# Two plain feed-forward blocks by token half, and the activation sums on GpSimd

## The chip, the core and the metric

The kernel runs on one NeuronCore of a Trainium2 chip. The metric is the device time of one execution in microseconds; the time given is the median of the runs. A change of 0.2% is about what the measurement can tell from no change.

## The reference

One layer of a diffusion backbone over 1024 latent tokens of width 1024 (and 256 context tokens). A modulated RMS norm and a projection feed two groups of heads, a bidirectional gated DeltaNet and a neighbourhood attention; their outputs go through one projection and a gated residual. The last part, which this case is about, is a second modulated RMS norm and a SwiGLU feed-forward with inner width 2816, with another gated residual:

```
x = x + g1 * (jnp.concatenate([dn_x, na_x], axis=-1) @ w_out[i])
x = x + g2 * swiglu(modulate(rms_norm(x, norm2_w[i]), sh2, sc2), w_ffn_in[i], w_ffn_out[i])

def swiglu(h, w_in, w_out):
    gate, up = jnp.split(h @ w_in, 2, axis=-1)
    return (jax.nn.silu(gate) * up) @ w_out
```

All inputs are float32.

## The kernel before

Activations are kept transposed: 128 partitions hold 128 of the 1024 features, the free axis holds tokens. The 1024 tokens are two halves of 512 (HV), because one matmul output is a bank of 128x512. Products of float32 values are made from rounded parts: every operand is split into hi (rounded, made on ScalarE) and lo (the rest, a subtraction on VectorE), and a product is three matmuls, hi*hi, hi*lo and lo*hi. A helper, product (L1206), issues for one weight pair and one 512x512 quarter of the activations 4 x 3 x 2 = 24 matmuls of 128x512 into two banks (L1212).

The normed activations form a 2x2 grid of quarters B11, B12, B21, B22: the first index is the half of the features, the second the half of the tokens. quadrant (L1394) makes one quarter: four times a scaling by weight and norm factor on VectorE (L1398), a shift on ScalarE (L1399), and the split (L1391 on ScalarE, L1392 on VectorE). The norm factor rs of a token half comes from normed (L1303): a matmul with ones over the sum of squares (L1306), then a logarithm and an exponential on ScalarE (L1307, L1308), each with a table load. finish (L1296) adds the last two feature rows of the residual for one half and updates the sum of squares (L1328, L1333, L1334).

The feed-forward's 22 blocks of 128 inner columns use two schemes. The first two blocks (PLAIN = 2) take gate and up columns with the quarters directly: eight products of 24 matmuls, in the order block 0 first half, block 0 second half, block 1 first half, block 1 second half. The other twenty go in pairs through a seven-product scheme on the 2x2 grid (L1491 to L1524), which needs four more activation tiles T1 to T4, sums of the quarters. sums (L1402) makes these while the second plain block runs: sixteen 128x512 subtractions (L1410, in place in the unsplit quarters) and their splits. T4 takes the buffers of B12.

Weights come through Stream: a raw tile wq by DMA on SyncE's queue (L1245), for some a sum ws of raw tiles on VectorE (L1269), then the pair uhi (ScalarE, L1273) and ulo (VectorE, L1274), six buffers each. make produces one pair; next takes two, gate and up; ahead(n) makes pairs until n are waiting. Around the plain blocks, a background generator, late, steps the modulation of the last gate (L231, L233, loads of wad) on VectorE; its result is used after the seven-product blocks. In the plain blocks, activation and product of gate and up are L1463 (ScalarE, SiLU) and L1464 (VectorE, reading the banks in PSUM).

The source order is not the order on the engines. The Tile framework traces the program and then schedules it: each engine gets its own order, from source priority and estimated ready times, with waits on the tiles' producers and on the last readers of a buffer that is used again. On the chip every engine then runs its own list in order.

## Time and profile before

| | us |
|---|---|
| median of 3 runs | 1626.84 |
| lowest and highest run | 1625.8, 1627.12 |
| profiled execution | 1629.29 |
| its span, first to last instruction | 1627.4 |
| mean granted TensorE clock | 0.974 |

The profile is of one execution. PE is TensorE's matmuls, PEld its weight loads, DVE VectorE, ACT ScalarE, POOL GpSimd, SPq SyncE's queue of DMA issues. Times in a timeline are from the start of the span; a bracket at the end of a row gives the idle time of the engine before it and what ended that. In a group of instructions, the numbers behind the bar are busy time, mean length of one in nanoseconds, and idle time before.

### The profile page before, as it was taken

How to read it: one execution, taken by the hardware profiler on the slowest of the kernel's cores; microseconds unless marked ns; L12 is line 12 of the kernel's file. 1: busy time of each engine (PE TensorE's matmuls, PEld its weight loads, DVE VectorE, ACT ScalarE, POOL GpSimd, SP SyncE). 2: the span in 40 equal slices, each digit the busy share in tenths (PEclk: the TensorE clock that was granted, in tenths of full speed). 3: DMA queues.
4: the chain of work that ended last, by engine and by line, in shares of the span. 5: the costliest groups of instructions: out<-in, count | busy, mean ns of one | idle time of the engine just before them, and what ended most of it. 6: DMA issues, size and time to landing. Idle time of an engine off the chain costs nothing.

```text
span 1627.4 us, 24128 instructions
## 1 busy us (share of the span) xinstructions
PE 1518.4 (93%) x8642; PEld 1278.9 (79%) x8642; DVE 1044.0 (64%) x1935; ACT 706.3 (43%) x1337; POOL 199.5 (12%) x271
## 2 busy tenths in 40 slices
PE   2999899999988897999998999999999999999999
PEld 1789787779888785788776787888888888888887
DVE  4785678544364466577897638876665666679752
ACT  4443363663332234565665227333333333445441
POOL 0144611422333320000010000000000000000000
PEclk9898999999999899999998999999999999999999
DMA  9266121545345537999955910533222323698742
GB/s 371 85 214 211 56 75 40 179 125 188 104 139 199 175 102 200 310 283 286 269 168 160 312 70 33 181 111 104 98 97 97 110 98 118 226 361 308 260 158 84
DMA packets 211719, 275.22 MB, mean 169 GB/s; under 512 B 16144, under 2 KB 120080, under 8 KB 210576
## 3 DMA queue, kind: packets, MB, share of 16 engines
q1 hardware_dynamic: 205552, 268.34, 51.0%
q10 hardware_dynamic: 6048, 5.35, 1.0%
q8 instruction: 68, 1.11, 0.3%
q14 instruction: 51, 0.42, 0.1%
HBM read 206.78 MB, written 71.04 MB: 171 GB/s over the span
## 4 chain that ended last, share of the span: by engine, by line
PE 74%; DVE 10%; DMA 7%; ACT 5%; issue 2%; POOL 2%; SPq 0%; ACTq 0%; DVEq 0%; POOLq 0%
PE ps L1212 26%; PE ps L1559 13%; PE blk L388 10%; PE blk L571 4%; PE ps L1343 3%; PE pr L913 3%; PE sc L317 2%; PE sc L307 2%; PE sc L295 2%; DMA wad<-wa 1%; DVE N L819 1%; DMA at<-qk_d 1%; DVE tt L817 1%; PE ps L1105 1%; PE pr L904 1%
## 5 line engine op out<-in xcount | busy, mean ns | idle before, releaser
L388 PE MATMUL blk<-hh,whi 128*128 128x512 f32 (+1 forms) x416 | 124.4, 391 | 3.6 <-ACT hh L683 3.3
L1273 ACT CAST uhi<-ws 128x512 fp32r<-128x512 f32 x91 | 54.7, 622 | 151.2 <-PE ps L1212 76.8
L1273 ACT CAST uhi<-wq 128x512 fp32r<-128x512 f32 x101 | 60.6, 621 | 136.0 <-issue 61.3
L388 PE MATMUL blk<-hh,wlo 128*128 128x512 f32 (+1 forms) x416 | 118.5, 378 | 0.6 <-POOL wlo L199 0.6
L388 PE MATMUL blk<-hl,whi 128*128 128x512 f32 (+1 forms) x416 | 117.9, 376 | 0.9 <-DVE hl L685 0.9
L1274 DVE TENSOR_TENSOR ulo<-wq,uhi 128x512 fp32r<-128x512 f32 x101 | 67.4, 688 | 66.7 <-ACT uhi L1273 35.6
L1212 PE MATMUL ps<-hT,uhi 128*128 128x512 f32 x336 | 104.6, 393 | 3.1 <-ACT hT L1391 3.1
L1212 PE MATMUL ps<-lT,uhi 128*128 128x512 f32 x336 | 104.0, 391 | 0.0
L1212 PE MATMUL ps<-hT,ulo 128*128 128x512 f32 x336 | 103.9, 390 | 0.0
L1212 PE MATMUL ps<-hB,uhi 128*128 128x512 f32 x288 | 89.7, 392 | 0.0
L571 PE MATMUL blk<-zhi,hh 128*128 128x256 f32 (+2 forms) x304 | 89.5, 294 | 0.0
L1212 PE MATMUL ps<-lB,uhi 128*128 128x512 f32 x288 | 89.3, 391 | 0.0
L1212 PE MATMUL ps<-hB,ulo 128*128 128x512 f32 x288 | 89.1, 390 | 0.0
L571 PE MATMUL blk<-zhi,hl 128*128 128x256 f32 (+2 forms) x304 | 88.2, 290 | 0.0
L571 PE MATMUL blk<-zlo,hh 128*128 128x256 f32 (+2 forms) x304 | 87.4, 288 | 0.0
L388 PEld LDWEIGHTS blk<-hh,wlo 128*128 128x128 f32 x416 | 73.9, 192 | 16.0 <-issue 1.6
L388 PEld LDWEIGHTS blk<-hl,whi 128*128 128x128 f32 x416 | 74.0, 193 | 15.5 <-DVE hl L685 1.2
L388 PEld LDWEIGHTS blk<-hh,whi 128*128 128x128 f32 x416 | 71.9, 195 | 17.6 <-issue 3.6
L1274 DVE TENSOR_TENSOR ulo<-ws,uhi 128x512 fp32r<-128x512 f32 x91 | 60.8, 687 | 37.5 <-ACT uhi L1273 29.2
L198 ACT CAST whi<-wraw 128x1024 fp32r<-128x1024 f32 x26 | 27.3, 1049 | 119.1 <-PE blk L388 56.9
L1212 PEld LDWEIGHTS ps<-hT,uhi 128*128 128x128 f32 x336 | 63.3, 189 | 16.5 <-ACT hT L1391 3.5
L1212 PEld LDWEIGHTS ps<-hT,ulo 128*128 128x128 f32 x336 | 63.4, 189 | 13.3
(331 smaller groups left out, 3751.9 us busy)
## 6 DMA issues: line engine op xcount, KB each, us to landing
wq<-w_fo SPq DMA_DIRECT2D x99, 256.0 KB
wq<-w_gu SPq DMA_DIRECT2D x88, 256.0 KB
wad<-wa SPq DMA_DIRECT2D x64, 256.0 KB
bt<-rpb SPq DMA_DIRECT2D x64, 192.0 KB
t_d<-g SPq DMA_DIRECT2D x22, 512.0 KB
fr<-t_d SPq DMA_DIRECT2D x44, 256.0 KB
f_d<-g SPq DMA_DIRECT2D x33, 256.0 KB
fr<-f_d SPq DMA_DIRECT2D x33, 256.0 KB
```

What stands on the lines that cost most here:

```text
L198: act.copy(h, r)
L295: pe.matmul(sc[:, u * 640 + n0:u * 640 + n1], q, ks[i], start=i == 0, stop=i == 1)
L307: pe.transpose(sc[:, u * 640 + j * 128:u * 640 + (j + 1) * 128], bt[:, j * 128:(j + 1) * 128], ident)
L317: pe.matmul(sc[u * ND:u * ND + ND, 1280:1408], vv, pt[:, j * 128:(j + 1) * 128], start=j == 0, stop=j == 4)
L388: pe.matmul(o, ww[:, k], xx[k][:, s], start=k == 0 and j == 0, stop=k == KT - 1 and j == 2)
L571: pe.matmul(p[:, :c1 - c0], x[k][:, s], ww[:, k, c0:c1], start=k == 0 and j == 0, stop=k == KT - 1 and j == 2)
L913: pe.matmul(p[:, hs[h]], f[:, h], src[:, h], start=True, stop=True)
L1212: pe.matmul(o, w[wi][:, k], x[xi][:, k], start=first and k == 0 and j == 0, stop=k == n - 1 and j == 2, skip_group_check=True)
L1273: act.copy(hi, self.raw[key])
L1274: dve.tensor_tensor(lo, self.raw[key], hi.bitcast(F32), OP.subtract)
L1343: pe.matmul(o, w[wi][:, k], parts[xi][k][:, s], start=k == 0 and j == 0, stop=k == KT - 1 and j == 2)
L1559: pe.matmul(o[b], w[wi][:, b], F[xn, p][xi], start=n in (0, 1, 5) and p == 0 and j == 0, stop=p == NFB // 2 - 1 and j == 2, skip_group_che ...
```

## The change

The two plain blocks are run by token half: both blocks over the first half, then both over the second. The ones-matmul for the second half's norm factor is issued inside the second product, after its first quarter, and the quarters B12 and B22 are made after the first block's first half, as before. All eight weight pairs of the two blocks stay in their buffers until the second half has used them, so uhi and ulo get eight buffers each instead of six; the space that the kernel reserves for DMA descriptors shrinks to 1024 bytes. The sixteen subtractions that make T1 to T4 go from VectorE to GpSimd; their splits stay on ScalarE and VectorE. They are issued beside the four products of the second half. The background modulation takes no steps in the first pair of the seven-product blocks.

```
-    def product(outs, ws, x, first=True):
+    def product(outs, ws, x, first=True, between=None):
...
+            if between and k == 0:
+                between()
...
-            hi = uw.tile([128, 4, 128], F32R, name="uhi", tag="uhi", bufs=6)
-            lo = uw.tile([128, 4, 128], F32R, name="ulo", tag="ulo", bufs=6)
+            hi = uw.tile([128, 4, 128], F32R, name="uhi", tag="uhi", bufs=8)
+            lo = uw.tile([128, 4, 128], F32R, name="ulo", tag="ulo", bufs=8)
...
-                    dve.tensor_tensor(B[at][:, k], B[x][:, k], B.get(y, B["B11"])[:, k], OP.subtract)
+                    pool.tensor_tensor(B[at][:, k], B[x][:, k], B.get(y, B["B11"])[:, k], OP.subtract)
...
-        for f in range(PLAIN):
-            po = [[bank(), bank()] for _ in range(2)]
-            g = prev[f]
-            w = [up.next(), None]
-            for t in range(2):
-                for i in range(2):
-                    if f == 0 and t == 1 and i == 0:
-                        for n in ("B12", "B22"):
-                            quadrant(n)
-                    if t == 0 and i == 1:
-                        w[1] = up.next()
-                    product([po[0][t], po[1][t]], w[i], X[f"B{i + 1}{t + 1}"], i == 0)
-                    if f == 0 and t == 0:
-                        if i == 0:
-                            normed(1)
-                        up.ahead(4)
-                    elif f:
-                        for _ in range(4):
-                            next(todo, 0)
-                        up.ahead(4)
-                act.activation(g[:, t], po[0][t], AF.Silu)
-                dve.tensor_tensor(g[:, t], po[1][t], g[:, t], OP.mult)
+        w = [[], []]
+        for t, f in ((0, 0), (0, 1), (1, 0), (1, 1)):
+            po, g = [bank(), bank()], prev[f]
+            for i in range(2):
+                if t == 0:
+                    w[f].append(up.next())
+                product(po, w[f][i], X[f"B{i + 1}{t + 1}"], i == 0,
+                        (lambda: normed(1)) if (t, f, i) == (0, 0, 1) else None)
+                if t == 0 and f == 0:
+                    up.ahead(2 + 2 * i)
+                elif t == 0 and i == 0:
+                    up.ahead(2)
+                elif t == 1:
+                    for _ in range(4):
+                        next(todo, 0)
+                    up.ahead(4 if f else 2)
+            act.activation(g[:, t], po[0], AF.Silu)
+            dve.tensor_tensor(g[:, t], po[1], g[:, t], OP.mult)
+            if t == 0 and f == 0:
+                for n in ("B12", "B22"):
+                    quadrant(n)
...
-                elif n % 2:
+                elif n % 2 and f > PLAIN:
                     late.step()
...
-    nc = bacc.Bacc("TRN2", target_bir_lowering=False, num_devices=1)
+    nc = bacc.Bacc("TRN2", target_bir_lowering=False, num_devices=1, dynamic_dma_scratch_size=1024)
```

## The prediction

> **What bounds the kernel now.** I read the page first, then busy time by windows around the edited stage, then the chain of waits, then the instruction timelines of TensorE, VectorE and GpSimd. The page says which engine is full:

> ```profile
> span 1627.4 us, 24128 instructions
> ...
> PE 1518.4 (93%) x8642; PEld 1278.9 (79%) x8642; DVE 1044.0 (64%) x1935; ACT 706.3 (43%) x1337; POOL 199.5 (12%) x271
> ...
> q1 hardware_dynamic: 205552, 268.34, 51.0%
> q10 hardware_dynamic: 6048, 5.35, 1.0%
> ```

> TensorE (PE) is busy 93% of the span, so a change can only win where PE is not. The feed-forward's two plain blocks run from 979.47 (first matmul of L1212) to 1031.19 (first matmul of block 2). In the windows the columns are: stretch and length, busy time and instructions of PE, PEld, DVE, ACT, POOL, then the granted clock, DMA share and GB/s.

> ```profile
> 979.47:1031.19 51.72, 47.81 (x197) 38.42 (x195) 46.55 (x76) 36.59 (x61) 0.00 (x0) 0.93 0.09 31
> 1031.19:1244.00 212.81, 212.81 (x944) 176.32 (x942) 137.46 (x217) 75.19 (x137) 0.00 (x0) 1.00 0.38 126
> ...
> 985.13:986.09 0.96, 0.16 (x1) 0.03 (x1) 0.96 (x3) 0.00 (x0) 0.00 (x0) 1.00 0.01 2
> 992.50:995.77 3.27, 0.16 (x1) 0.00 (x0) 2.73 (x5) 2.43 (x5) 0.00 (x0) 0.82 0.00 0
> 995.77:1001.47 5.70, 5.70 (x13) 4.51 (x14) 5.70 (x11) 5.69 (x9) 0.00 (x0) 0.50 0.14 49
> 1001.47:1031.19 29.72, 29.72 (x133) 24.59 (x131) 27.31 (x46) 17.60 (x32) 0.00 (x0) 1.00 0.08 27
> ```

> From 1031.19 on PE is busy for the whole stretch at full clock: time won before that point is kept. Inside the plain blocks there are two holes, 0.96 and 3.27 us, and behind the second one 5.70 us in which PE is busy but the granted clock is 0.50. VectorE is busy 46.55 of 51.72 us here, and GpSimd not at all. What ends the second hole is in the chain of waits (start, length, what), and the pace of PE on either side of it in its timeline:

> ```profile
> 989.08 1.28 ACT L1307
> 992.38 0.64 ACT rs L1308
> 993.04 0.76 DVE x L1398
> 993.83 1.39 ACT x L1399 x2
> 995.21 0.52 ACT hT L1391
> 995.77 247.74 PE ps L1212 x1080
> ...
> 986.09 1.10 PE L1306 MATMUL ps<-acc,ones 128*128 128x512 f32 x2 [0.80 <-DVE acc L1334]
> 986.63 1.03 PE L1212 MATMUL ps<-hB,uhi 128*128 128x512 f32 x2
> 987.49 0.63 PE L1212 MATMUL ps<-lB,uhi 128*128 128x512 f32 x2
> 996.79 1.06 PE L1212 MATMUL ps<-hB,uhi 128*128 128x512 f32 x2
> 1031.19 0.62 PE L1212 MATMUL ps<-hB,uhi 128*128 128x512 f32 x2
> 1042.07 0.62 PE L1212 MATMUL ps<-hT,uhi 128*128 128x512 f32 x2
> 1047.51 0.62 PE L1212 MATMUL ps<-hB,uhi 128*128 128x512 f32 x2
> ```

> The second hole waits for the second token half: its norm factor (rs, done at 993.0), then scale, shift and rounding of the first quarter of B12. The first hole waits for the sum of squares that the ones-matmul of L1306 reads. The row of 996.79 shows products of B11 (second block, first half of the tokens) already mixed in behind the hole: the instruction order is not the source's order, the builder schedules it.

> Pace: 1031.19 to 1047.51 holds three products of 24 matmuls, 16.32 us, so 5.44 us each. The eight plain products need 43.5 us. The pair of L1306 and the next pair take 987.49 - 986.09 = 1.40 us, 0.95 beyond the 0.45 of an ordinary pair. Floor 44.5 of 51.72 us: 7.2 lost. The parts are 0.96 + 3.27 us of holes, and 5.70 us at clock 0.50, half of which (2.85) is lost: 7.1.

> **The change, part by part.**

> *Order of the two blocks.* The second block's first-half products (10.9 us, tiles B11 and B21, long since made) now stand between the first block's first half and the first product with B12. From the row of 979.47: 5.44 for B11, 1.36 for the first quarter of B21, 0.95 for L1306 now placed there, 4.08 for the rest of B21, 10.88 for block 1: B12 is wanted at about 1002.2 instead of 992.5. The chain that delivered its first quarter at 995.77 does not start later, so the 3.27 us hole goes, and the 2.85 us of half clock with it. What hides the norm chain is those 10.9 us of products; without them it costs 6.1 us again. B22 is wanted 5.44 us later, at 1007.6, its last quarter at 1011.7.

> *The ones-matmul inside B21's product.* It needs the last add of L1334, and comes at 986.27 in the new order:

> ```profile
> 985.26 0.68 DVE L1334 TENSOR_TENSOR acc<-acc,ws 128x512 f32<-128x512 f32 x1
> 989.00 1.28 DVE L1392 TENSOR_TENSOR lB<-x,hB 128x512 fp32r<-128x512 f32 x2
> 1002.60 1.29 DVE L1392 TENSOR_TENSOR lB<-x,hB 128x512 fp32r<-128x512 f32 x2
> 1008.99 0.69 DVE L1392 TENSOR_TENSOR lB<-x,hB 128x512 fp32r<-128x512 f32 x1
> 1032.57 0.68 DVE L1274 TENSOR_TENSOR ulo<-ws,uhi 128x512 fp32r<-128x512 f32 x1
> ```

> The add ends at 985.94, so the 0.96 us hole goes, with only 0.3 us to spare. The next thing late is B21's third quarter: its lo part comes from the row of 989.00 (first of two, about 989.6), PE wants it at 989.0. Cost 0 to 0.6, taken as 0.4. The gain so far: 0.96 + 3.27 + 2.85 - 0.4 = 6.7 us.

> *The sixteen sums T1 to T4 on GpSimd.* This is where the change can give its gain back. No row shows such a subtraction there, so I bound it by the nearest ones, and look at what VectorE does beside GpSimd:

> ```profile
> L1410 DVE TENSOR_TENSOR x<-x 128x512 f32<-128x512 f32 x16 | 10.3, 686 | 0.0
> L199 DVE TENSOR_TENSOR wlo<-wraw,whi 128x1024 fp32r<-128x1024 f32 x8 | 9.7, 1218 | 0.4 <-ACT whi L198 0.4
> L199 POOL TENSOR_TENSOR wlo<-wraw,whi 128x1024 fp32r<-128x1024 f32 x18 | 43.6, 2420 | 191.4 <-ACT whi L198 172.1 <-ACT WK L831 14.0 <-PE blk L388 5.0
> L879 POOL TENSOR_TENSOR rg<-GH,cst 128x512 fp32r<-128x512 f32 x20 | 21.1, 1055 | 34.4 <-PE pr L889 34.0
> ...
> 79.75 2.40 POOL L199 TENSOR_TENSOR wlo<-wraw,whi 128x1024 fp32r<-128x1024 f32 x1 [33.76 <-ACT whi L198]
> 80.47 2.22 DVE L233 SCALAR_TENSOR_TENSOR acc<-wad,sc,acc 128x512 f32<-128x512 f32 x1
> 1054.87 0.75 DVE L233 SCALAR_TENSOR_TENSOR acc<-wad,sc,acc 128x512 f32<-128x512 f32 x1
> ...
> 171.41 1.05 POOL L775 TENSOR_TENSOR rc<-GH,cst 128x512 fp32r<-128x512 f32 x1 [4.66 <-DVE gY L739]
> 183.16 2.30 POOL L775 TENSOR_TENSOR rc<-GL,cst 128x512 fp32r<-128x512 f32 x1
> ```

> One sum costs at least 1.05 us (L879, same size, broadcast operands); half of L199's 2.42 is 1.21; and 0.686 times the ratio of L199 on the two engines (2.42/1.218) is 1.36. I take 1.2, the half of the row with full operands. That is 19.2 us on GpSimd, which has nothing else queued in this stretch (0.00 x0), against 11.0 on VectorE. Behind each sum wait ScalarE's cast of L1391 and, queued after it there, the casts of the next weights. It is no clean transfer: the operation of L233 takes 0.75 us alone (1054.87) but 2.22 when it starts inside GpSimd's operation of 79.75, and ends half a microsecond after it. The same L775 takes 1.05 alone and 2.30 where VectorE runs two-operand work. The two engines take turns. [...]

> Does that reach PE? B22's first quarter was done at about 1003.2 (first of the pair of 1002.60), its last at 1009.68 (1008.99); it has 4.4 and 2.0 us to spare. Four T1 sums can push in front (4.8 us), three VectorE sums leave that stretch (2.1 us), and the rounding of the second block's late weights, for which ScalarE and VectorE stood waiting on PE, no longer waits since there are eight buffers. Taken as hidden, with about one to two microseconds of cover; without it up to 2 us.

> The tightest consumer is the third product of block 2, whose summed weights S2 are made behind the T4 splits on VectorE: done at 1033.26 (1032.57), used at 1042.07, 8.8 us spare. VectorE's work from 979.47 to there is 46.55 + 2.1 = 48.6 us of 53.8. New: 48.6 - 11.0 + 19.2 = 56.8, less about 2.8 for the four products of L1464, which read PSUM and can run beside GpSimd: 54.0 us, and about one us of idle that stays. PE asks for S2 at 44.9 + 10.9 = 55.8 us after 979.47. So 0.8 us to spare with 1.2 us a sum, 3.2 with 1.05, 1.8 us late with 1.36. I book 0.6 us.

> *Edits with one answer.* Eight weight buffers cost only space; the 1024-byte DMA scratch frees it, and the page's queue rows are all hardware queues, so nothing waits on that scratch. The modulation steps taken out of block 2 are VectorE operations of 0.75 us (L233) moved to later blocks, where VectorE is busy 137 of 212.8 us and PE is never idle: nothing. Count of table loads, matmuls and DMAs is unchanged.

> Sum: -7.1 + 0.4 + 0.6 = -6.1 us. The profiled execution took 1629.29 us (span 1627.4 and 1.9 around it), 2.45 above the median of the runs; the same difference is taken off both: 1623.2 for a like execution, **1620.7** for the median. What a measurement of this kernel can tell from no change is 0.2%, 3.25 us.

> **The rivals.**

> *The shared path takes most of it.* At 1.36 us a sum, or with sums that wait for the lo splits of the sum before, S1 and S2 come 3 to 5 us late: -6.7 + 4 = -2.7, about 1624 (1623 to 1627). This is the case in which taking turns binds at every sum. For it: the slack of 0.8 us is a difference of large numbers. Against it: in the rows from 183.16 a turn of both engines takes less than their separate times.

> *Slower.* The same sums, but the wait at S2 (or at B22) reaches the length that drops the clock. The 3.27 us hole did, and cost 2.85 more. It decides from about 1.45 us a sum on the shared path, (0.8 + 3.3)/16 = 0.25 above what I took. With a 6 us wait: -6.7 + 6 + 2.85 = +2.2, 1629. [...] For it: the 2.30 us rows. Against it: those contain a whole VectorE operation that also got done.

> *It does not do what it says.* The builder already ran second-block products among B12's (996.79), so it may place B12's first quarter at the same spot: the hole stays, 1626.8. Against it: B12 now stands behind these products in the source.

> *Placement.* Eight more KB of weights and fifteen less of scratch move tiles to other addresses, and with them which freed tile an earlier load waits for. No row prices it; a few microseconds either way.

> **How the numbers follow.** Forecast 0.52 (1619 to 1623.5 by the bounds of the sum), the shared path 0.18, slower 0.17, no effect 0.07, placement 0.06. Faster by over 0.2%: 0.52, four tenths of the second case (0.07) and half of the last: 0.62. Slower: 0.17 and half the last, 0.20. Within: 0.18. The range runs from 1618 (full 7.1 and a little of placement) to 1629.5 (the slower case).

> **What would show it.** Right: no PE hole over 0.6 us between 979 and 1024, clock 1.00 in the stretch, block 2 starting near 1025; second-block B11 products directly behind B21's first; sixteen GpSimd subtractions near 1.2 us, longer where VectorE works. Wrong: PE waiting on ulo (L1274 of before) in block 2, a wait for hB or hT at the first product of the second half, or a stretch at 0.50 after 1024; or a shift of the stages ahead of 979.

## The result: slower, by 9 us where 6 were to be won

| | before | after |
|---|---|---|
| median of 6 runs each, us | 1626.96 (1625.8 to 1628.85) | 1636.15 (1634.42 to 1643.94) |
| ratio to before | 1 | 1.0056 [1.0038, 1.0074] |
| profiled execution, us | 1629.29 | 1643.94 |
| its span, us | 1627.4 | 1642.1 |

The forecast was 1620.7 us (1618.0 to 1629.5). Of the 14.7 us between the two spans 7.6 arise ahead of the feed-forward; a second execution of the changed kernel (e9 below) does not have them. The other 7.1 are the subject here. The ratios below leave out one execution, of 5466 us among the ten of e11, over three times as long as any other.

The page of after, lines that answer to those shown of before:

```profile
span 1642.1 us, 24112 instructions
...
PE 1523.0 (93%) x8642; PEld 1281.0 (78%) x8642; DVE 1052.0 (64%) x1919; ACT 706.5 (43%) x1337; POOL 227.0 (14%) x287
...
q1 hardware_dynamic: 205552, 268.34, 50.3%
```

Sixteen instructions have gone from VectorE to GpSimd, and GpSimd is busy 27.5 us longer. Busy time by windows of after (columns as in the prediction): the two plain blocks, block 2, the blocks behind it, and two pieces inside block 2.

```profile
987.31:1032.97 45.66, 45.03 (x195) 36.21 (x194) 42.90 (x46) 32.67 (x54) 26.04 (x16) 1.00 0.07 24
1032.97:1084.00 51.03, 42.26 (x170) 33.07 (x169) 43.96 (x69) 16.89 (x31) 0.66 (x1) 0.90 0.47 154
1084.00:1245.00 161.00, 161.00 (x712) 133.32 (x711) 98.88 (x155) 56.16 (x102) 0.00 (x0) 1.00 0.34 115
1068.72:1075.68 6.96, 0.00 (x2) 0.00 (x1) 6.82 (x12) 2.78 (x5) 0.00 (x0) 0.67 0.38 125
1075.68:1081.85 6.17, 6.17 (x15) 4.65 (x16) 6.13 (x11) 1.85 (x3) 0.00 (x0) 0.55 0.11 42
```

And block 2 of before by the same view:

```profile
1031.19:1069.30 38.11, 38.11 (x170) 31.56 (x169) 33.40 (x53) 13.71 (x26) 0.00 (x0) 1.00 0.63 207
```

The plain blocks take 45.66 us instead of 51.5 (from the first matmul at 979.69; the prediction's 979.47 is that matmul's weight load). This is most of the gain that was forecast, 5.8 us of 6.7. Block 2 takes 51.03 instead of 38.11: 12.9 lost. The timeline of TensorE in after shows where; these are all its rows with a wait from 985 to 1090:

```profile
997.35 0.73 PE L1212 MATMUL ps<-lB,uhi 128*128 128x512 f32 x2 [0.38 <-DVE lB L1394]
1014.21 0.74 PE L1212 MATMUL ps<-lT,uhi 128*128 128x512 f32 x2 [0.25 <-DVE lT L1394]
1034.84 1.10 PE L1212 MATMUL ps<-hB,ulo 128*128 128x512 f32 x2 [0.80 <-DVE ulo L1276]
1046.40 0.99 PE L1212 MATMUL ps<-hT,uhi 128*128 128x512 f32 x2 [0.92 <-ACT e L1508]
1075.68 1.45 PE L1212 MATMUL ps<-hT,uhi 128*128 128x512 f32 x2 [6.96 <-DVE e L1517]
```

The last is the seventh product of block 2, with T4. It accumulates into bank pair b1, and must not start before VectorE's sum e35 (L1517 of after, L1515 of before) has read that bank. It waits 6.96 us, and then runs 6.17 us at a mean clock of 0.55, which loses 0.45 of it, 2.8 us. With the other two waits of block 2 (1.72) that is 11.5 of the 12.9; the rest lies mostly in the first pairs of matmuls behind these two waits, which take 1.10 and 0.99 us instead of 0.62.

Why e35 is late stands in the chain of waits of after (start, length, what) and in VectorE's timeline there:

```profile
1048.17 4.03 DMA wq<-w_gu
1052.24 0.70 DVE g L1437
1053.89 3.95 DMA wad<-wa
1057.99 0.68 DVE ulo L1276
1058.67 0.68 DVE acc L233
...
1060.15 4.75 DMA wad<-wa
...
1075.02 0.61 DVE e L1517
1075.68 14.36 PE ps L1212 x50
```

```profile
1041.33 2.48 DVE L1394 TENSOR_TENSOR lT<-x,hT 128x512 fp32r<-128x512 f32 x4
1048.06 0.48 DVE L231 TENSOR_SCALAR acc<-wad,sc 128x512 f32<-128x512 f32 x1
1057.32 0.75 DVE L233 SCALAR_TENSOR_TENSOR acc<-wad,sc,acc 128x512 f32<-128x512 f32 x1 [3.19 <-DMA wad<-wa]
1063.59 0.69 DVE L1271 TENSOR_TENSOR ws<-wq 128x512 f32<-128x512 f32 x1 [1.17 <-DMA wq<-w_gu]
1068.07 3.11 DVE L233 SCALAR_TENSOR_TENSOR acc<-wad,sc,acc 128x512 f32<-128x512 f32 x4
1071.09 1.28 DVE L1514 TENSOR_TENSOR g<-ps,e 128x512 f32<-128x512 f32 x2
1074.94 1.28 DVE L1517 TENSOR_TENSOR e<-ps,e 128x512 f32<-128x512 f32 x2
```

Between the splits of T4 (1041.33) and e35 stand the sixteen operations of the last gate's modulation (L231, L233). They multiply weights `wad` that come by DMA. VectorE takes them in the order of its list: it stands 3.19, 0.28 and 0.24 us for these loads, and e35 behind them starts at 1074.94, although TensorE had finished its bank at 1063.3 and ScalarE its other operand at 1050.3. The loads were themselves held up. SyncE's queue, in the view of waits:

```profile
SPq L212 <- DVE lT L1394: 20.5, 1, 20.5
```

The loads' tiles lie on space that the last T4 split sets free. That split ends at 1043.8, where the first load is issued. So the reading is: sums on GpSimd make T4's splits late, these make the loads late, these hold VectorE, and that holds T4's product until TensorE's clock drops (to 0.50 from 1071.0 on). The experiments take parts of this chain away.

### The profile page after: what moved, and what is told of

Its sections match the earlier page's. It is cut to its first block, busy times and chain, and to the rows that moved or that the text cites. A ratio compares the mean times of both kernels' runs of the same rounds, so it can differ in the third digit from the quotient of the medians.

```text
span 1642.1 us, 24112 instructions
## 1 busy us (share of the span) xinstructions
PE 1523.0 (93%) x8642; PEld 1281.0 (78%) x8642; DVE 1052.0 (64%) x1919; ACT 706.5 (43%) x1337; POOL 227.0 (14%) x287
## 3 DMA queue, kind: packets, MB, share of 16 engines
q1 hardware_dynamic: 205552, 268.34, 50.3%
q10 hardware_dynamic: 6048, 5.35, 1.0%
## 4 chain that ended last, share of the span: by engine, by line
PE 71%; DVE 13%; DMA 6%; ACT 5%; issue 3%; POOL 1%; SPq 1%; ACTq 0%; DVEq 0%
PE ps L1212 21%; PE ps L1561 13%; PE blk L388 11%; PE blk L571 4%; PE ps L1345 3%; PE pr L913 3%; PE sc L317 2%; PE sc L307 2%; PE sc L295 1%; DMA wad<-wa 1%; DVE N L819 1%; DVE tt L817 1%; PE pr L904 1%; DVE lT L1394 1%; PE ps L1105 1%
## 5 line engine op out<-in xcount | busy, mean ns | idle before, releaser
L388 PE MATMUL blk<-hh,whi 128*128 128x512 f32 (+1 forms) x416 | 125.5, 394 | 4.9 <-ACT hh L683 4.5
L388 PE MATMUL blk<-hl,whi 128*128 128x512 f32 (+1 forms) x416 | 119.7, 381 | 0.9 <-DVE hl L685 0.9
L1275 ACT CAST uhi<-ws 128x512 fp32r<-128x512 f32 x91 | 53.8, 620 | 153.4 <-PE ps L1212 86.5
L388 PE MATMUL blk<-hh,wlo 128*128 128x512 f32 (+1 forms) x416 | 119.1, 379 | 0.6 <-POOL wlo L199 0.6
L1212 PE MATMUL ps<-hT,uhi 128*128 128x512 f32 x336 | 105.4, 394 | 7.9 <-DVE e L1517 7.0
L1212 PE MATMUL ps<-lT,uhi 128*128 128x512 f32 x336 | 104.6, 392 | 0.3 <-DVE lT L1394 0.3
L1212 PE MATMUL ps<-hT,ulo 128*128 128x512 f32 x336 | 104.3, 392 | 0.0
L1212 PE MATMUL ps<-hB,ulo 128*128 128x512 f32 x288 | 89.0, 390 | 0.9 <-DVE ulo L1276 0.8
L1212 PE MATMUL ps<-lB,uhi 128*128 128x512 f32 x288 | 88.8, 389 | 0.4 <-DVE lB L1394 0.4
L1212 PE MATMUL ps<-hB,uhi 128*128 128x512 f32 x288 | 89.1, 391 | 0.0
L388 PEld LDWEIGHTS blk<-hh,wlo 128*128 128x128 f32 x416 | 74.8, 195 | 16.4 <-issue 1.6
L388 PEld LDWEIGHTS blk<-hl,whi 128*128 128x128 f32 x416 | 75.1, 196 | 15.9 <-DVE hl L685 1.2
L388 PEld LDWEIGHTS blk<-hh,whi 128*128 128x128 f32 x416 | 72.3, 196 | 18.9 <-ACT hh L683 4.6
L1212 PEld LDWEIGHTS ps<-hT,uhi 128*128 128x128 f32 x336 | 63.6, 190 | 22.4 <-DVE e L1517 7.4
L198 ACT CAST whi<-wraw 128x1024 fp32r<-128x1024 f32 x26 | 27.3, 1049 | 118.9 <-PE blk L388 57.1
L1212 PEld LDWEIGHTS ps<-lT,uhi 128*128 128x128 f32 x336 | 63.6, 189 | 13.9 <-DVE lT L1394 0.7
L1212 PEld LDWEIGHTS ps<-hT,ulo 128*128 128x128 f32 x336 | 63.6, 189 | 13.4
```

The source lines that it names most:

```text
L198: act.copy(h, r)
L388: pe.matmul(o, ww[:, k], xx[k][:, s], start=k == 0 and j == 0, stop=k == KT - 1 and j == 2)
L1212: pe.matmul(o, w[wi][:, k], x[xi][:, k], start=first and k == 0 and j == 0, stop=k == n - 1 and j == 2, skip_group_check=True)
L1275: act.copy(hi, self.raw[key])
```

## The experiments

Two marks cut each trace: the first matmul of L1212, and the first matmul of the feed-forward's third block. All times are of the profiled execution, one of each kernel; the ratio is of all runs against before on the same chip.

| kernel | first mark at | mark to third block | third block to end | ratio |
|---|---|---|---|---|
| before | 979.7 | 89.6 | 558.1 | |
| after | 987.3 | 96.7 | 558.1 | 1.0056 [1.0038, 1.0074] |
| e1 sums on VectorE | 978.9 | 84.9 | 558.1 | 0.9985 [0.996, 1.0011] |
| e2 old order, sums on GpSimd | 983.0 | 92.7 | 558.2 | 1.0045 [1.0024, 1.0065] |
| e3 no modulation | 975.9 | 86.7 | 556.2 | 0.9994 [0.9974, 1.0015] |
| e4 space only | 979.0 | 88.3 | 558.1 | 0.9996 [0.9975, 1.0018] |
| e5 modulation early | 981.5 | 86.7 | 556.4 | 0.9992 [0.997, 1.0015] |
| e6 early, sums on VectorE | 981.0 | 83.2 | 556.2 | 0.996 [0.9936, 0.9984] |
| e7 no loads | 980.4 | 88.2 | 558.2 | 0.9986 [0.9965, 1.0008] |
| e8 before, modulation early | 982.0 | 87.0 | 556.7 | 0.9991 [0.9969, 1.0013] |
| e9 after again | 979.3 | 97.4 | 558.1 | 1.0039 [1.0018, 1.006] |
| e10 before again | 982.0 | 89.7 | 558.1 | 0.9993 [0.9969, 1.0016] |
| e11 T1, T2 on GpSimd | 978.0 | 92.9 | 558.1 | 1.0015 [0.9992, 1.0038] |
| e12 T3, T4 on GpSimd | 987.8 | 93.9 | 558.1 | 1.004 [1.0015, 1.0065] |

The last part is the same 558.1 to 558.2 us for every kernel with the modulation in its place, so nothing is won or lost there.

**e1, the sums back on VectorE** (all else as after).

```
-  pool.tensor_tensor(B[at][:, k], ..., OP.subtract)
+  dve.tensor_tensor(B[at][:, k], ..., OP.subtract)
```

> The new order with the sixteen sums back on VectorE. Theory (GpSimd's sums and VectorE take turns, T4's splits come some 12 us late, and the queue of VectorE behind them reaches TensorE at the last product of block 2): TensorE has no wait over 1 us in block 2, the plain blocks still take about 45.7 us, and the time is 1619 to 1622. Rival (the new order alone brings TensorE too early for VectorE's work): the 7 us wait before the product with T4 stays, 1633 to 1637.

84.9 us between the marks instead of 96.7. In TensorE's timeline T4's product waits 1.01 us (and 0.18 one matmul later):

```profile
1057.88 0.50 PE L1212 MATMUL ps<-hT,uhi 128*128 128x512 f32 x1 [1.01 <-DVE e L1517]
```

In VectorE's, the last T4 split, the first modulation operation and e35:

```profile
1026.53 0.69 DVE L1394 TENSOR_TENSOR lT<-x,hT 128x512 fp32r<-128x512 f32 x1
1035.56 0.48 DVE L231 TENSOR_SCALAR acc<-wad,sc 128x512 f32<-128x512 f32 x1
1057.14 1.28 DVE L1517 TENSOR_TENSOR e<-ps,e 128x512 f32<-128x512 f32 x2
```

So the loss needs the sums on GpSimd, and the reordering wins 4.7 us against before (89.6), of which up to 2.9 are the half clock behind before's hole, which varies (see the end). By the time of all runs (median 1629.14 us, above the 1619 to 1622 expected) the gain is not to be told from none.

**e2, the old order with the sums on GpSimd** (the same one word changed in before).

> The old order with only the sixteen sums moved to GpSimd. Theory: the sums cost as much here, TensorE comes 6 us later, so part of the delay is covered: 1629 to 1636, with a wait in block 2 behind VectorE, mostly before the product with T4. Rival (order): no change, 1626 to 1628.

92.7 us, and no wait in block 2, where the theory had put it. The sums cost here in the plain blocks; TensorE's waits there:

```profile
999.08 1.22 PE L1212 MATMUL ps<-hT,uhi 128*128 128x512 f32 x2 [3.11 <-ACT hT L1391]
1002.45 1.22 PE L1212 MATMUL ps<-lT,uhi 128*128 128x512 f32 x2 [0.44 <-DVE lT L1392]
1009.83 0.73 PE L1212 MATMUL ps<-lT,uhi 128*128 128x512 f32 x2 [1.89 <-DVE lT L1392]
```

The first hole is before's own; the second and third are new. The sums on GpSimd lose in either order (here by the runs too, ratio 1.0045), at another consumer in each.

**e3, after without the last gate's modulation.** Its sixteen loads, sixteen VectorE operations and the reductions behind them are left out; the gate takes the values that scale the second norm.

```
-  late.add(modulation(pools(us, "adp", "left"), range(6, 8), bank))
+  dve.tensor_copy(modp[:, 40:48], modp[:, 32:40])
```

> The changed kernel without the background modulation of the last gate: its 16 loads, 16 VectorE operations and their two reductions are left out, and the gate takes the values of another row. Theory in full (VectorE's queue stands on the late modulation loads in front of the sums of block 2): the 7 us wait before T4 goes, 1625 to 1629. If VectorE is late by GpSimd alone, without the modulation: at least half of the wait stays, 1631 to 1635.

86.7 us; the wait ahead of T4's product is gone, the waits of 0.81 (ulo) and 0.93 (e) in block 2 remain. So the sums need the modulation to do their full harm.

**e4, before with eight weight buffers and the 1024-byte scratch.**

> The kernel before with eight weight buffers and the small DMA scratch, nothing else. Theory: no effect on the plain blocks, 1626 to 1628. Rival (placement, or two more weight pairs made in front of the output projection): the stage before 979 grows by 2 to 5 us, 1629 to 1632.

88.3 us. The 1.3 us to before are the length of the half-clock stretch behind the same 3.11 us hole (see the end). Space costs and gives nothing that can be told.

**e5 and e6, the modulation moved ahead.** Its operations now stand beside the output projection, in after (e5) and in e1 (e6).

```
-  late.add(modulation(pools(os_, "adp", "left"), range(4, 6), bank))
+  late.add(modulation(pools(os_, "adp", "left"), range(4, 8), bank))
...
-  if b and k % 2:
+  if b:
...
-  late.add(modulation(pools(us, "adp", "left"), range(6, 8), bank))
```

> The changed kernel, sums on GpSimd, with the last gate's modulation stepped beside the output projection instead of block 2. Theory (the wait before T4 needs both GpSimd's sums and the modulation queued in front of block 2's sums on VectorE): no wait over 2 us in block 2; from the first plain matmul to the end of the span 642 to 645 us (654.8 in the changed kernel, 647.7 in the one before). Rival (GpSimd's sums alone keep VectorE late): a wait of 3 us or more before T4 stays, 648 to 653. The output projection may grow by 0 to 4 us for 16 more loads.

> The new order, sums on VectorE, and the modulation beside the output projection. Theory: no wait over 0.5 us in block 2; first plain matmul to the end 641 to 643 us, the best of all; time 0.1 to 0.5% below the kernel before. Rival (output projection pays for the loads): it grows by 4 us or more and nothing is won.

From the first mark to the end e5 takes 643.1 us and e6 639.4, with 654.8 for after and 647.7 for before. In e6 TensorE waits once, 0.39 us, from the first mark to the end of block 2. It is the only version here that is faster than before by its runs: median 1623.23 us, ratio 0.996 [0.9936, 0.9984]. Not all of the 8.3 us is kept: its output projection takes 100.3 us from first matmul to first mark, where after takes 97.9 and before 96.0 and, again, 98.1.

The four kernels with the new order make a square: 83.2 (sums on VectorE, modulation early), 86.7 (GpSimd, early), 84.9 (VectorE, in place), 96.7 (GpSimd, in place). The sums alone cost 3.5, the modulation in place alone 1.7, both together 13.5: more than 8 us come from their meeting, of which 2.8 are the dropped clock.

**e7, after without the modulation's loads.** The sixteen operations stay, but read a constant tile; the last gate's values are therefore others.

```
-            if order:
+            if resident is not None:
+                landing.append(resident)
+            elif order:
...
-        late.add(modulation(pools(us, "adp", "left"), range(6, 8), bank))
+        late.add(modulation(pools(us, "adp", "left"), range(6, 8), bank, fixed))
```

> The changed kernel with the last gate's modulation computed from a tile that is already there: its 16 VectorE operations stay in the queue, its 16 loads are left out, and the gate has other values. Theory in full (VectorE stood about 5 us on late loads): the 7 us wait before T4 falls to 0 to 3 us; first plain matmul to the end 644 to 650 us. Rival (it is VectorE's own work): 5 us or more of the wait stays, over 651.

88.2 us, 646.4 to the end. GpSimd's sums are as slow as in after (mean 1.70 us, its group), but T4's product waits only 0.49 and 0.19 us (TensorE's timeline):

```profile
L1416 POOL TENSOR_TENSOR x<-x 128x512 f32<-128x512 f32 x16 | 26.7, 1696 | 141.6 <-ACT x L1405 139.1 <-DVE lT L1398 2.4
```

```profile
1062.57 0.50 PE L1216 MATMUL ps<-hT,uhi 128*128 128x512 f32 x1 [0.49 <-DVE e L1521]
```

So it is the loads that carry it, not the VectorE time of the operations. From the end of the last T4 split to e35 VectorE has the same 39 operations in after and in e7. Busy time in these two stretches (columns as in the prediction), of after and of e7:

```profile
1043.81:1074.94 31.13, 23.99 (x104) 19.00 (x102) 24.45 (x39) 10.87 (x20) 0.00 (x0) 0.94 0.74 245
```

```profile
1036.86:1061.83 24.97, 23.82 (x104) 19.03 (x102) 23.44 (x39) 9.79 (x19) 0.00 (x0) 1.00 0.42 137
```

VectorE is idle for 6.7 us of the first and 1.5 of the second, so 5.2 of the 6.2 us between them are waits (in after for loads of `wad`, 3.7 us, for a store, 1.5, and for a weight load, 1.2). Leaving out the loads changes two more things: the operations stand elsewhere in the queue (the first 57.0 us behind the first mark, 60.8 in after), and SyncE's queue no longer stands 20.5 us for a T4 split. These were not tried apart.

**e8, before with the modulation early.**

> The kernel before with the modulation moved beside the output projection, nothing else. Theory: TensorE never waits in block 2 there, so nothing is won: first plain matmul to the end 646 to 648 us, time 1626 to 1632 with the output projection 0 to 4 us longer. Rival (modulation costs TensorE by itself): 2 us or more faster.

87.0 us, 643.7 to the end: less than expected, and by the number alone the rival's. But of the 4.0 us to before 2.6 lie between the marks, where the hole of the plain blocks is there (3.16 us) and the clock did not drop behind it; 1.4 lie behind the third block. The move by itself is therefore not shown to win anything on the way to T4's product, and its ratio says the same.

**e9 and e10, both kernels again.**

> The changed kernel once more, unchanged. Measured from the first matmul of the feed-forward to the first of its third block, the earlier executions gave 89.6 us (before) and 96.7 us (after); from there to the end both took 558.1. If the loss lies between these two marks, this execution gives 95 to 98 us there, with the wait of about 7 us ahead of the last product of block 2, whatever the time up to the first mark is (979.7 us before, 987.3 after, 976 to 983 in the others). The rival, that the loss lies in the stages ahead of the feed-forward, needs the first mark at 985 to 989 again; if it comes at 978 to 983, what the profiled execution lost ahead of the mark was a matter of that execution. Time by the first theory: about 7 us over the kernel before, ratio 1.003 to 1.006.

> The kernel before, unchanged, timed as if it were another kernel. Ratio 1.000 with an interval of about 0.002 to each side, which says how small a difference these comparisons can tell. From the first matmul of the feed-forward to the first of its third block 87 to 90 us: 3.2 us of hole ahead of the first B12 product each time, and 0 to 3 us lost to the half clock behind it.

After again has 97.4 us between the marks, with 7.8 us ahead of T4's product, and its first mark is at 979.3: the 7.6 us that the first profile of after lost ahead of the mark are a matter of that execution (e12 has its mark as late, at 987.8). Before again has 89.7 us, and against before a ratio of 0.9993 [0.9969, 1.0016].

**e11 and e12, half of the sums on GpSimd.**

```
-  pool.tensor_tensor(...)
+  (pool if n in ("T1", "T2") else dve).tensor_tensor(...)
```

This is e11; e12 has T3 and T4 in the place of T1 and T2.

> The changed kernel with the sums T1 and T2 on GpSimd and T3 and T4 on VectorE. Theory one (VectorE's in-order queue as a whole is late, each sum on GpSimd delays it by about one microsecond, wherever the sum stands): half the delay, so 88 to 91 us between the two marks (85.0 with all on VectorE, 96.7 with all on GpSimd), and a wait of 2 to 4 us ahead of block 2's last product. Rival (only the sums that stand last, T3 and T4, delay it, since the first ones have slack to be absorbed): 85 to 86 us, wait about 1 us.

> The changed kernel with the sums T3 and T4 on GpSimd and T1 and T2 on VectorE. Theory one (every sum counts the same): 88 to 91 us between the marks, wait of 2 to 4 us ahead of block 2's last product, no waits at the T1 products. Rival (only the last sums delay it): 92 to 97 us, the wait of about 7 us in full.

Between the marks 92.9 and 93.9 us; ahead of T4's product 6.24 and 7.44 us. Half the sums, of either kind, give nearly the whole wait. Theory one's numbers missed in both runs; the rival's came in e12 and missed in e11. GpSimd's group in e11, and in e12:

```profile
L1412 POOL TENSOR_TENSOR x<-x 128x512 f32<-128x512 f32 x8 | 13.2, 1679 | 146.7 <-ACT x L1401 138.1 <-DVE lT L1394 8.6
```

```profile
L1412 POOL TENSOR_TENSOR x<-x 128x512 f32<-128x512 f32 x8 | 18.2, 2298 | 150.0 <-ACT hB L1393 145.0 <-DVE lT L1394 5.0
```

The rows of VectorE's timeline in e11 that answer to those of e1:

```profile
1028.18 2.49 DVE L1394 TENSOR_TENSOR lT<-x,hT 128x512 fp32r<-128x512 f32 x4
1034.92 0.48 DVE L231 TENSOR_SCALAR acc<-wad,sc 128x512 f32<-128x512 f32 x1
1061.42 1.28 DVE L1517 TENSOR_TENSOR e<-ps,e 128x512 f32<-128x512 f32 x2
```

Counted from each kernel's first mark:

| us behind the first mark | e1 (none) | e11 (T1, T2) | e12 (T3, T4) | after (all) |
|---|---|---|---|---|
| last T4 split ends | 48.3 | 52.6 | 53.6 | 56.5 |
| first load of `wad` issued | 48.3 | 52.7 | 53.6 | 56.5 |
| first modulation operation | 56.6 | 56.9 | 57.8 | 60.8 |
| e35 starts | 78.2 | 83.4 | 85.2 | 87.6 |
| T4's product could start, but for e35 | 77.9 | 77.9 | 78.6 | 81.4 |

The first two lines go by halves, as theory one has it, and agree to 0.1 us in every kernel: the split does release the load. From the split to e35 it is nearly the same time in all four, 29.9 to 31.6 us, although it is made up differently: in e1 VectorE comes to the modulation 8.3 us after the first load and needs 21.6 us from its first operation to e35, in the other three 4.2 to 4.3 and 26.5 to 27.4, with two of the sums of L1434 to L1437, which e1 has ahead of the modulation, between its operations. So e35 is later than in e1 by 5.2, 7.0 and 9.4 us, and 4.3, 5.3 and 8.2 of these are the split's delay.

The last line says why half the sums still give nearly the whole wait: in after TensorE is itself 3.5 us later at T4's product than in e1, mostly by the two earlier waits of block 2, which e11 and e12 do not have. So the split's delay goes roughly by the number of sums, as theory one says; the wait that TensorE shows does not.

## Why the prediction was wrong

**Right: what the order wins.** The two holes and the half clock of the plain blocks went (5.8 us by the windows, 6.7 forecast). Two small waits stand in their place, 0.38 and 0.25 us; B21's lo part, booked at 0.4, is the first of them.

**Right: what the sums cost VectorE.** Forecast 1.2 us each, 19.2 in all. GpSimd's group of sums in after, its timeline, and VectorE's:

```profile
L1412 POOL TENSOR_TENSOR x<-x 128x512 f32<-128x512 f32 x16 | 26.7, 1698 | 142.1 <-ACT x L1401 139.7 <-DVE lT L1394 2.4
```

```profile
1020.06 13.58 POOL L1412 TENSOR_TENSOR x<-x 128x512 f32<-128x512 f32 x8 [2.44 <-DVE lT L1394]
```

```profile
1022.80 11.38 DVE L1394 TENSOR_TENSOR lT<-x,hT 128x512 fp32r<-128x512 f32 x7
```

Eight sums in 13.58 us are 1.70 each, and the seven VectorE splits of the same time take 1.63 each where four take 2.48 (0.6 each) without GpSimd. The reading is that a sum and a split take turns, so that 0.6 of the 1.70 is the split and 1.10 the sum. That is near the low bound of the prediction (1.05), and it is below the 1.45 us a sum on the shared path (the two engines' work, one after the other) from which the slower case was to decide. The forecast's 19.2 us in place of 11.0 come to 8.2 us more on that path, and the last T4 split does end 8.2 us later in after than in e1 (56.5 against 48.3). That the two figures are equal is luck: sixteen turns with 1.10 in place of the 0.6 that VectorE takes come to 8.0, and the forecast had 1.2 and 0.69. The 2.8 us that the forecast took off for the four products of L1464, because they read PSUM, were an estimate without a row; in after two of the four (L1463 there, at 1008.37 and 1022.20) start while GpSimd is at a sum and take 0.68 us, and the two outside (1037.11, 1045.66) take 0.68 and 0.69. So VectorE was as late as forecast; what failed is the account of what stands behind it.

**Wrong: that S2 is the tightest consumer.** The slack of 8.8 us was worked out for the third product of block 2, and that product was not late for its weights (0.92 us, for ScalarE's copy). The tightest consumer is the bank of the seventh. In before e35 is done 0.4 us ahead of the product that overwrites its bank; the timelines of VectorE and then of TensorE of before:

```profile
1062.14 1.28 DVE L1515 TENSOR_TENSOR e<-ps,e 128x512 f32<-128x512 f32 x2
```

```profile
1063.83 0.61 PE L1212 MATMUL ps<-hT,uhi 128*128 128x512 f32 x2
```

TensorE busy without a gap from 1031.19 on was read as room. It was a stretch with 0.4 us to spare at one point, and the prediction looked for waits on operands only, not for a bank that has to be read first. Two of its own signs of being wrong showed: a wait on `ulo` in block 2 (0.80 us) and a stretch at about half clock behind 1024 (0.55).

**Wrong: that the modulation steps move to later blocks and cost nothing.** The source's condition moved, the instructions did not. The tile `wad` in after:

```profile
L233 DVE SCALAR_TENSOR_TENSOR acc<-wad,sc,acc x14: 743/752/753, 1048.6 to 1074.3; 128x512 f32<-128x512 f32 x14
L212 SPq DMA_DIRECT2D wad<-wa x16: 327/358/821, 1043.8 to 1069.6; - x16
```

All sixteen still run in block 2, ahead of e35 in VectorE's queue; before has them at 1039.3 to 1061.5. The builder orders the instructions, as the prediction itself had read off the row of 996.79. Where the modulation really was moved (e5 against e6), the sums cost 3.5 us and not 11.8.

**The rival that came nearest** was "slower": same sums, a wait of about 6 us, then the half clock, +2.2 us. Its course and both prices were near (6.96 us and 2.8), but it was put at S2 or B22, it was to need 1.45 us a sum on the shared path, which was not reached, and it was given 0.17. In its terms the measured sum is -5.8 + 7.0 + 2.8, and to these 4.0 us come the 1.7 us of small waits in block 2 and the 1.4 us that lie mostly in the slow pairs behind them: 7.1.

**The space** was nothing, as forecast (e4, ratio 0.9996).

## What to carry to other kernels

Before moving work from VectorE to GpSimd beside operations of VectorE like the splits here, count one turn as the sum of both durations (0.6 for a split and 1.10 for a sum made 1.70 us in after; the first sum of e12, at the end, is an exception), and follow the delay down VectorE's whole queue: not to the consumer of the moved result alone, but to whatever stands behind it, the release of PSUM banks included. Work that waits for a DMA and stands ahead in the same in-order queue uses up the room that would have taken up the delay; with the sums on GpSimd, moving that work away won back 10.0 of the 11.8 us that they cost (e5). And whether a step has moved is read from the trace's instruction order, not from the source.

## What the runs showed of the hardware

The same hole of 3.10 to 3.16 us ahead of the first T product has different consequences. Windows of the hole and the 6.4 us behind it (length, PE busy, clock, DMA share, GB/s) in before again (e10), then of e4 (the stretch behind the hole) and of e8:

```profile
995.01:998.11 3.10, 0.00 (x1) 0.84 0.00 0
998.11:1004.51 6.40, 6.40 (x16) 0.54 0.12 44
```

```profile
995.06:1001.46 6.40, 6.40 (x22) 0.76 0.12 44
```

```profile
994.95:998.11 3.16, 0.01 (x1) 1.00 0.00 0
998.11:1004.51 6.40, 6.40 (x28) 1.00 0.11 41
```

GpSimd's sums took 1.68 us in the mean in e11 and, with one exception, about 1.7 each in e12 (shortest, median, longest):

```profile
L1412 POOL TENSOR_TENSOR x<-x x8: 1672/1734/6351, 1010.4 to 1031.9; 128x512 f32<-128x512 f32 x8
```

The exception, the first sum of e12, took 6.35 us, and it alone lifts the mean there to 2.30 us. While it was open, VectorE did nine operations at its usual pace of 0.6 us. So the two engines do not always take turns one by one; what decides it was not tried.
